# Three small edits in a two-layer recurrent and attention step: a weight remainder split one unit later, a norm's root by ScalarE, and three of four last scalings on VectorE

## The chip, the core and the metric

One core of a Trainium2 chip runs the whole program. Times are device microseconds of one execution. TensorE (PE) multiplies, VectorE (DVE), ScalarE (ACT) and GpSimd (POOL) do the elementwise work, each executing its own queue in order, and SyncE (SP) issues most DMAs. What counts is the median time of several executions of the program.

## What is computed

The reference is one step of a streaming encoder with two layers, in float32. Per layer:

```python
z = rms_norm(h, norm_w) @ w_in            # 8 parts of 1024 columns
o_r = rglru(xr, zr)                       # 8 independent blocks of 128 channels
o_a = diff_attention(q, k, v, za)         # 8 heads
h = h + (sigmoid(g_r) * (o_r @ w_proj_rnn) + sigmoid(g_a) * (o_a @ w_proj_att)) @ w_out
```

The recurrent branch (RG-LRU) of one block of 128 channels:

```python
xc = causal_conv(xr)                      # 4 taps
r = sigmoid(xc @ w_rg + b_rg); i = sigmoid(xc @ w_ig + b_ig)
a = exp(-8 * r * softplus(-lru_lambda))
h[t] = a[t] * h[t-1] + sqrt(1 - a[t]**2) * i[t] * xc[t]
```

At the end the rows of `h` go through a last `rms_norm` to `y_prompt` (512 tokens) and `y_sample` (64 tokens).

## The kernel before

Activations are kept transposed: 128 channels on the partitions, 592 tokens (64 sample, 16 meta, 512 prompt) along the row. Each float32 product is made of three matmuls on rounded parts: a weight `w` is split into `wh` (rounded copy, ACT, line 156) and `wl` (the rest, DVE or POOL, line 161), and data likewise.

`dense` (line 196) makes one block of 128 output channels. It works in two halves of 296 (or 288) tokens, and one such half, 24 matmuls, is called a unit here: about 3.3 us of PE. After a unit's matmuls the code hands its PSUM bank to an evacuation, then calls `step()`, then splits weights some pieces ahead. `step()` advances every generator in the list `active` to its next `yield`, the oldest generator first. The generators hold everything that runs beside the dense products, so each engine's queue is written out by hand: what stands earlier in a step stands earlier in the queue.

`rnn_steps` (line 762) is the generator of one RG-LRU block. Its stages, one for each unit, are called U0 to U13 here:

- U0: the gate weights `gw` are loaded by DMA; POOL makes the first tap of the convolution (`xc`, line 769) and two copies of three columns (lines 770 and 771).
- U1 to U3: DVE adds the other taps (line 774).
- U4: ACT rounds `xc` to `xh` (line 779) and `gw` to `gh` (line 780); POOL makes the rest `gl` (line 781).
- U5: DVE makes the rest `xl` (line 783).
- U6 and U7: PE makes the two gates, six matmuls each in the order `gh*xh`, `gh*xl`, `gl*xh` (line 790), and ACT takes their tanh (line 792).
- U8: ACT makes Exp, Tanh and Sqrt (lines 797 to 799), DVE a product (line 800).
- U9: DVE makes `a` (line 802), POOL finishes it (line 803).
- U10 and U11: DVE (lines 805 and 807).
- U12: DVE scans over time (lines 810 and 811), POOL copies two last states (lines 812 and 813).
- U13: DVE multiplies by the gate (line 817).

`chains()` (line 853) starts the next block four units or more after the last one, so U4 of a block falls into the step of U0 of the next, U5 into that of U9 of the block before and of U1 of the next, and U12 of a block into that of U4 of the second block after it. Blocks are numbered 0 to 7 in the first layer and 8 to 15 in the second. Before each block of `xr` POOL also fills the border columns of `xb` (lines 889 to 892).

The last stage of layer 1 multiplies by `w_out` in two parts, of 320 and of 256 tokens. Per block, DVE adds the residual (`hn`, line 1068) and scales it (`hx`, line 1069), ACT squares it (line 1074), POOL sums the squares (line 1076), and `to_tokens` (line 1027) transposes `hx` on PE and lets ACT copy the transposed block to `Y` (line 1034). After the second part `sums` (line 286) multiplies the two remaining sums, `acc` and the last `sq`, by ones on PE to get one sum of squares per token, all into one bank; `rstd` (line 281) makes the inverse root on DVE from a magic number and three Newton steps (lines 267 to 273); and `scale_out` (line 1042) scales `Y` and sends it out by DMA, in four pieces of 128 tokens x 512 columns: two on DVE with SP's queue, two on ACT with ACT's own queue.

Of the kernel before, what the change touches and what calls it, by code (L numbers as in the profile page):

```python
# [26 lines left out]
AF = mybir.ActivationFunctionType  # L27
OP = mybir.AluOpType
AX = mybir.AxisListType

D = 1024
# [6 lines left out]
EPS = 1e-6  # L38
# [8 lines left out]
def f32(ap):  # L47
    return ap.bitcast(FT)
# [39 lines left out]
def tile_kernel(ctx, tc, I, O):  # L88
    nc = tc.nc
    V, S, P, PE, SY = nc.vector, nc.scalar, nc.gpsimd, nc.tensor, nc.sync  # L90
# [19 lines left out]
    def ps_t():  # L110
        return ps.tile([128, 512], FT, name="pt")

    def ps_s():
        return ps.tile([128, 2, 512], FT, name="pss", bufs=2)
# [4 lines left out]
    def small(name, n, dt=FT, bufs=2):  # L119
        return sm.tile([128, n], dt, name=name, bufs=bufs)  # L120
# [110 lines left out]
    ones = cn.tile([128, 128], FT, name="ones")  # L231
# [49 lines left out]
    def rstd(ss, n=5, E=V):  # L281
        v = small("v5", 5)[:, :n]
        E.tensor_scalar(v, ss, 1.0 / D, EPS, op0=OP.mult, op1=OP.add)
        return rsqrt(v, n, E)

    def sums(xs, tiles, p=None, between=None):

        p = p or ps_t()
        for t, (c, n) in enumerate(tiles):
            for i, x in enumerate(xs):  # L290
                PE.matmul(p[:n, t:t + 1], x[:, c:c + n], ones[:, 0:1], start=(i == 0), stop=(i == len(xs) - 1))
        full = [t for t, (c, n) in enumerate(tiles) if n == 128]
        assert full == list(range(len(full)))
        if len(full) == len(tiles):
            return rstd(p[:, :len(tiles)], len(tiles))
        ss = small("ssl", 5)[:, :len(tiles)]
        V.memset(ss, 1.0)
        V.tensor_copy(ss[:, :len(full)], p[:, :len(full)])
        for t in range(len(full), len(tiles)):
            n = tiles[t][1]  # L300
            V.tensor_copy(ss[:n, t:t + 1], p[:n, t:t + 1])
        if between:
            between()
        return rstd(ss, len(tiles))
# [23 lines left out]
    def conv_w(l, k, j): return prm[:, 16 + 32 * l + 8 * k + j:16 + 32 * l + 8 * k + j + 1]  # L328
    def conv_b(l, j): return prm[:, 80 + 8 * l + j:80 + 8 * l + j + 1]
    def state_rnn(l, j): return prm[:, 144 + 8 * l + j:144 + 8 * l + j + 1]  # L330
    def state_conv(l, k, j): return prm[:, 160 + 24 * l + 8 * k + j:160 + 24 * l + 8 * k + j + 1]
    def half_brg(l, j): return hb[:, 8 * l + j:8 * l + j + 1]
    def half_big(l, j): return hb[:, 16 + 8 * l + j:16 + 8 * l + j + 1]
    def sp_m4(l, j): return spc[:, 0, 8 * l + j:8 * l + j + 1]
    def sp_p2(l, j): return spc[:, 1, 8 * l + j:8 * l + j + 1]
# [74 lines left out]
    for k in range(KT):  # L410
# [10 lines left out]
        for n in range(2):  # L421
            for i, (a, b) in enumerate(((0, hwh), (0, hwl), (1, hwh))):
                for hf, (c0, m) in enumerate(ALL):
                    PE.matmul(banks[n][hf][:, :m], wt[n][a][:, k], b[k][:, c0:c0 + m], start=(k == 0 and i == 0),  # L424
                              stop=(k == KT - 1 and i == 2))
# [336 lines left out]
    def rnn_steps(l, j, xb, zg, orr, NSt, rp):  # L762
        def rblk(name, dt=FT):
            return rp.tile([128, TW], dt, name=name, tag="r", bufs=9)

        gw = rp.tile([128, 2, 128], FT, name="gw", bufs=2)
        SY.dma_start(gw, I["gw"][l, j])
        xc = rblk("xc")
        P.tensor_scalar(xc, xb[:, 0:TW], conv_w(l, 0, j), conv_b(l, j), op0=OP.mult, op1=OP.add)
        P.tensor_copy(NSt[:, 0, j:24:8], xb[:, 528:531])  # L770
        P.tensor_copy(NSt[:, 1, j:24:8], xb[:, 595:598])
        for k in range(1, 4):
            yield
            V.scalar_tensor_tensor(xc, xb[:, k:k + TW], conv_w(l, k, j), xc, op0=OP.mult, op1=OP.add)
        yield
        gh = rp.tile([128, 2, 128], FR, name="gh", bufs=2)
        gl = rp.tile([128, 2, 128], FR, name="gl", bufs=2)
        xh, xl = rblk("xh", FR), rblk("xl", FR)
        S.activation(xh, xc, AF.Copy)
        S.activation(gh, gw, AF.Copy)  # L780
        P.tensor_tensor(gl, gw, f32(gh), op=OP.subtract)
        yield
        V.tensor_tensor(xl, xc, f32(xh), op=OP.subtract)
        yield
        tg = []
        for g, bias in ((0, half_brg(l, j)), (1, half_big(l, j))):
            p = ps_s()
            for i, (w, x) in enumerate(((gh, xh), (gh, xl), (gl, xh))):
                for hf in range(2):
                    PE.matmul(p[:, hf, :298], w[:, g], x[:, 298 * hf:298 * hf + 298], start=(i == 0), stop=(i == 2))  # L790
            t = rblk(f"tg{g}")
            S.activation(t.rearrange("p (a b) -> p a b", a=2), p[:, :, :298], AF.Tanh, bias=bias, scale=0.5)
            tg.append(t)
            yield
        v, u = tg
        e, q, a = rblk("e"), rblk("q"), v
        S.activation(e, v, AF.Exp, bias=sp_m4(l, j), scale=sp_m4(l, j))
        S.activation(v, v, AF.Tanh, bias=sp_p2(l, j), scale=sp_p2(l, j))
        S.activation(q, v, AF.Sqrt)
        V.scalar_tensor_tensor(u, u, 1.0, xc, op0=OP.add, op1=OP.mult)  # L800
        yield
        V.scalar_tensor_tensor(a, e, 1.0, v, op0=OP.add, op1=OP.mult)
        P.tensor_scalar(a, a, -1.0, 1.0, op0=OP.mult, op1=OP.add)
        yield
        V.scalar_tensor_tensor(e, e, 1.0, q, op0=OP.add, op1=OP.mult)
        yield
        V.scalar_tensor_tensor(u, e, 0.5, u, op0=OP.mult, op1=OP.mult)
        hs = e
        yield
        V.tensor_tensor_scan(hs[:, 0:528], a[:, 0:528], u[:, 0:528], 0.0, op0=OP.mult, op1=OP.add)  # L810
        V.tensor_tensor_scan(hs[:, 531:595], a[:, 531:595], u[:, 531:595], state_rnn(l, j), op0=OP.mult, op1=OP.add)
        P.tensor_copy(NSt[:, 0, 24 + j:25 + j], hs[:, 527:528])
        P.tensor_copy(NSt[:, 1, 24 + j:25 + j], hs[:, 594:595])
        yield
        o = orr[j] = rp.tile([128, T], FT, name="or", bufs=4) if j < 4 else blk("or")
        for c, n, t0 in (((0, 64, 531), (64, 528, 0)) if l == 0 else ((16, 64, 531), (80, 512, 16))):
            V.scalar_tensor_tensor(o[:, c:c + n], hs[:, t0:t0 + n], 0.5, zg[:, c:c + n], op0=OP.mult, op1=OP.mult)
# [11 lines left out]
    for l in range(DEPTH):  # L829
# [33 lines left out]
        for nm in order_rnn():  # L863
# [51 lines left out]
            if rp is None and not active:  # L915
# [5 lines left out]
                    lambda n, dt, i=i: rp.tile([128, T], dt, name=f"{n}{i}") for i in range(3)]))  # L921
# [96 lines left out]
        else:  # L1018
# [23 lines left out]
            def scale_out(t, y, i, E, q, c):  # L1042
                n = 64 if t == 4 else 128
                if E is S:
                    S.activation(Y[:n, t, c], Y[:n, t, c], AF.Copy, scale=y[:n, i:i + 1])
                else:
                    E.tensor_scalar(Y[:n, t, c], Y[:n, t, c], y[:n, i:i + 1], None, op0=OP.mult)
                dst = O["y_prompt"][0, 128 * t:128 * (t + 1), c] if t < 4 else O["y_sample"][0][:, c]
                q.dma_start(dst, Y[:n, t, c])

            def first_out(xs, tiles):
# [3 lines left out]
                for i, (t, c) in enumerate(tiles):  # L1055
                    scale_out(t, y, i, V, SY, slice(0, D))
                    yield

            for part, (c0, m, tiles) in enumerate(parts):
                acc = blk("acc")  # L1060
                xs = [acc]
                for j in range(KT):
                    load_h(part, j + 1)
                    hn, hx = blk("hn"), blk("hx")

                    def evac(hf, c0, m, p):
                        cs = slice(c0, c0 + m)
                        V.tensor_tensor(hn[:, cs], p[:, :m], hos[part, j][:, cs], op=OP.add)
                        V.tensor_scalar(hx[:, cs], hn[:, cs], fw[:, j:j + 1], None, op0=OP.mult)
                        if j == 0:  # L1070
                            S.activation(acc[:, cs], hn[:, cs], AF.Square)
                        else:
                            sq = blk("sq")
                            S.activation(sq[:, cs], hn[:, cs], AF.Square)
                            if j < KT - 1:
                                P.tensor_tensor(acc[:, cs], acc[:, cs], sq[:, cs], op=OP.add)
                            else:
                                xs.append(sq)

                    dense((l, f"out{'ab'[part]}{j}"), (mh, ml), evac, [(c0, m)])  # L1080
                    if part == 0 or j < KT - 1:
                        active.append(token_step(j, hx, tiles))
                if part == 0:
                    active.append(first_out(xs, tiles))
            y = sums(xs, [(c, 128) for t, c in tiles])
            to_tokens(KT - 1, hx, tiles)
            for g in range(2):
                c = slice(512 * g, 512 * g + 512)
                scale_out(2, y, 0, V, SY, c)
                scale_out(3, y, 1, S, S, c)  # L1090


_OUTS = [("y_prompt", (1, 512, 1024)), ("y_sample", (1, 64, 1024)), ("new_k", (DEPTH, NH, 128, T)),
# [76 lines left out]
```

## Time and profile before

| | |
|---|---|
| median of 3 runs | 1324.07 us (1323.75 to 1325.9) |
| the profiled execution | 1325.13 us |
| its span on the core | 1323.4 us |
| busy: PE, DVE, ACT, POOL | 1311.1, 969.1, 673.7, 375.7 us |
| matmuls | 9768 |

The span is what the profile of the core covers; the profiled execution takes 1.7 us more around it. Busy times are sums over all instructions of an engine; a matmul's end is modelled, so starts of successive matmuls say more of PE than its busy share.

### The profile page before, as it was taken

The page shows a single profiled execution, that of the slowest core. Times are in us where ns is not written, and L with a number is a line of the kernel's source. Part 1 is how long each engine was busy: PE and PEld are TensorE (multiplying, and loading weights), DVE is VectorE, ACT ScalarE, POOL GpSimd, SP SyncE. Part 2 cuts the span into 40 slices and gives each one's busy share as a digit, 9 for nine tenths or more (in the row PEclk, how much of TensorE's full clock was granted, in tenths as well). Part 3 has the DMA queues.
Part 4 walks back from the last instruction along what each step waited for, and adds up shares of the span by engine and source line. Part 5 has one row for each costly group of instructions (what it writes and reads, how often), then busy time and mean ns, then how long its engine had stood idle before and what let it go on. Part 6 is the DMA issues. An engine that isn't in the chain of part 4 may idle for free.

```text
span 1323.4 us, 26301 instructions
## 1 busy us (share of the span) xinstructions
PE 1311.1 (99%) x9768; PEld 1306.7 (99%) x9768; DVE 969.1 (73%) x2031; ACT 673.7 (51%) x1575; POOL 375.7 (28%) x736
## 2 busy tenths in 40 slices
PE   9999999999999999999999999999999999999997
PEld 9999999999999999999999999999999999999997
DVE  7998888874477886555568898998735789755576
ACT  5455555564336664423425555555632566553343
POOL 1224555442212331000212245445231143200011
PEclk9999999999999999999999999999999999999999
DMA  6557777776332221223443677777663222222254
GB/s 228 171 143 171 184 175 188 183 179 146 103 106 73 73 83 65 97 80 126 175 140 113 168 187 186 185 174 181 165 153 120 69 77 89 80 81 80 92 184 140
DMA packets 260575, 179.06 MB, mean 135 GB/s; under 512 B 177952, under 2 KB 222624, under 8 KB 260448
## 3 DMA queue, kind: packets, MB, share of 16 engines
q1 hardware_dynamic: 260016, 176.85, 47.5%
q8 instruction: 77, 1.26, 0.4%
q10 hardware_dynamic: 432, 0.53, 0.1%
q14 instruction: 50, 0.41, 0.1%
HBM read 132.37 MB, written 35.26 MB: 127 GB/s over the span
## 4 chain that ended last, share of the span: by engine, by line
PE 86%; issue 6%; DVE 3%; DMA 2%; POOL 1%; SPq 1%; ACT 0%; ACTq 0%; POOLq 0%; DVEq 0%
PE pd L208 72%; PE pss L478 2%; PE pss L481 2%; PE po L545 2%; PE pss L790 2%; PE pt L545 1%; DMA gw<-in_gw_dram 1%; PE pd L424 1%; DVE wl L161 1%; PE pt L543 1%; PE po L208 1%; PE pss L208 0%; PE pt L208 0%; PE pt L549 0%; PE pss L424 0%
## 5 line engine op out<-in xcount | busy, mean ns | idle before, releaser
L208 PE MATMUL pd<-hwh,wh 128*128 128x296 f32 (+1 forms) x1968 | 589.0, 299 | 1.4 <-DVE xs L664 1.3
L208 PE MATMUL pd<-hwh,wl 128*128 128x296 f32 (+1 forms) x1968 | 587.0, 298 | 0.7 <-DVE wl L161 0.7
L208 PE MATMUL pd<-hwl,wh 128*128 128x296 f32 (+1 forms) x1968 | 586.0, 298 | 0.0
L208 PEld LDWEIGHTS pd<-hwh,wh 128*128 128x128 f32 x1968 | 370.6, 188 | 2.0 <-DVE xs L664 1.1
L208 PEld LDWEIGHTS pd<-hwh,wl 128*128 128x128 f32 x1968 | 370.2, 188 | 1.2 <-DVE wl L161 1.2
L208 PEld LDWEIGHTS pd<-hwl,wh 128*128 128x128 f32 x1968 | 370.9, 188 | 0.0
L161 DVE TENSOR_TENSOR wl<-stg,wh 128x512 fp32r<-128x512 f32 x321 | 236.6, 741 | 0.3 <-ACT wh L156 0.2
L156 ACT ACTIVATE wh<-stg 128x512 fp32r<-128x512 f32 x364 | 221.7, 621 | 4.5 <-PE pss L208 1.6
L758 ACT ACTIVATE zg<-zt 128x296 f32<-128x296 f32 (+1 forms) x64 | 28.7, 449 | 157.6 <-DVE zt L757 151.2
L511 ACT ACTIVATE P<-pss,nm 128x400 f32<-128x400 f32 (+4 forms) x128 | 62.4, 492 | 81.8 <-DVE nm L508 78.0
L676 POOL TENSOR_TENSOR xc<-xc,xr 128x592 f32<-128x592 f32 x32 | 50.4, 1576 | 183.7 <-DMA xr<-xs 111.9
L161 POOL TENSOR_TENSOR wl<-stg,wh 128x512 fp32r<-128x512 f32 x43 | 59.6, 1386 | 112.1 <-ACT wh L156 100.7
L208 PE MATMUL pd<-oah,wl 128*128 128x296 f32 (+1 forms) x256 | 76.4, 298 | 0.8 <-DVE wl L161 0.8
L208 PE MATMUL pd<-mh,wh 128*128 128x296 f32 (+2 forms) x256 | 77.1, 301 | 0.0
L208 PE MATMUL pd<-oal,wh 128*128 128x296 f32 (+1 forms) x256 | 76.2, 298 | 0.0
L208 PE MATMUL pd<-mh,wl 128*128 128x296 f32 (+2 forms) x256 | 76.2, 298 | 0.0
L208 PE MATMUL pd<-orl,wh 128*128 128x296 f32 (+1 forms) x256 | 76.1, 297 | 0.0
L208 PE MATMUL pd<-oah,wh 128*128 128x296 f32 (+1 forms) x256 | 76.1, 297 | 0.0
L208 PE MATMUL pd<-orh,wl 128*128 128x296 f32 (+1 forms) x256 | 76.0, 297 | 0.0
L208 PE MATMUL pd<-orh,wh 128*128 128x296 f32 (+1 forms) x256 | 75.9, 296 | 0.0
L208 PE MATMUL pd<-ml,wh 128*128 128x296 f32 (+2 forms) x256 | 75.9, 296 | 0.0
L520 ACT ACTIVATE P<-pss,nm 128x528 f32<-128x528 f32 x32 | 22.5, 702 | 71.5 <-DVE nm L518 46.3
(262 smaller groups left out, 2545.7 us busy)
## 6 DMA issues: line engine op xcount, KB each, us to landing
stg<-in_w_dram SPq DMA_DIRECT2D x182, 512.0 KB, 3.7
pd<-AB SPq DMA_DIRECT2D x64, 160.0 KB, 3.7
PT<-pd SPq DMA_DIRECT2D x64, 160.0 KB, 3.7
xr<-xs SPq DMA_DIRECT2D x128, 74.0 KB, 4.3
od<-ob SPq DMA_DIRECT2D x64, 80.0 KB, 3.1
kv<-kv SPq DMA_DIRECT2D x64, 76.0 KB, 2.3
out_new_k_dram<-xc SPq DMA_DIRECT2D x16, 296.0 KB, 4.0
out_new_v_dram<-vT SPq DMA_DIRECT2D x16, 296.0 KB, 3.8
```

The costliest lines, as they stand in the source:

```text
L156: S.activation(hi, src, AF.Copy)
L161: E.tensor_tensor(lo, src, f32(hi), op=OP.subtract)
L208: PE.matmul(p[:, :m], a[:, k], b[k][:, c0:c0 + m], start=(i == 0), stop=(i == 23))
L424: PE.matmul(banks[n][hf][:, :m], wt[n][a][:, k], b[k][:, c0:c0 + m], start=(k == 0 and i == 0), stop=(k == KT - 1 and i == 2))
L478: PE.matmul(p[:nq, slot, :nn], qs[c][:, q0:q0 + nq], ks[c][:, k0:k0 + nn], start=True, stop=False)
L481: PE.matmul(p[:nq, slot, :nn], qlz[c][:, q0:q0 + nq], ks[c][:, k0:k0 + nn], start=False, stop=True)
L511: S.activation(pcs[i, cc][:nq, :n], p[:nq, cc, :n], AF.Exp, bias=nm[:nq, cc:cc + 1], accum_out=Z[:nq, cc, i:i + 1])
L520: S.activation(pcs[i, c][:, :528].rearrange("p (a b) -> p a b", a=2), p[:, :, :264], AF.Exp, bias=nm[:, :1], accum_out=Z[:, c, i:i + 1])
L545: PE.matmul(o, PT[0][:, j0 + j], vt[:, j], start=False, stop=(j == i))
L676: P.tensor_tensor(xc[x][:, :T], xc[x][:, :T], r[:, :T], op=OP.add)
L758: S.activation(zg[:, cs], zt[:, cs], AF.Tanh, scale=0.5)
L790: PE.matmul(p[:, hf, :298], w[:, g], x[:, 298 * hf:298 * hf + 298], start=(i == 0), stop=(i == 2))
```

## The change

`gl` is made by POOL in U5 instead of U4. In the last stage, a one-element Sqrt on ACT stands ahead of the two parts; the two last sums go to two banks of another PSUM tile, in the order acc, acc, sq, sq; the root of the last norm is ACT's Sqrt, DVE's reciprocal and one step of Newton; and three of the four last scalings are on DVE with SP's queue, one on ACT.

```diff
         S.activation(xh, xc, AF.Copy)
         S.activation(gh, gw, AF.Copy)
+        yield
         P.tensor_tensor(gl, gw, f32(gh), op=OP.subtract)
-        yield
         V.tensor_tensor(xl, xc, f32(xh), op=OP.subtract)
         yield
...
+            root = small("root", 1)
+            S.activation(root, ones[:, 0:1], AF.Sqrt)
             for part, (c0, m, tiles) in enumerate(parts):
...
-            y = sums(xs, [(c, 128) for t, c in tiles])
+            p = ps_s()
+            for i, x in enumerate(xs):
+                for t, (_, c) in enumerate(tiles):
+                    PE.matmul(p[:, t, 0:1], x[:, c:c + 128], ones[:, 0:1], start=(i == 0), stop=(i == 1))
             to_tokens(KT - 1, hx, tiles)
-            for g in range(2):
-                c = slice(512 * g, 512 * g + 512)
-                scale_out(2, y, 0, V, SY, c)
-                scale_out(3, y, 1, S, S, c)
+            v, y, a, b = [small(n, 2) for n in ("v5", "ny", "na", "nb")]
+            V.tensor_scalar(v, p[:, :, 0], 1.0 / D, EPS, op0=OP.mult, op1=OP.add)
+            S.activation(y, v, AF.Sqrt)
+            V.tensor_scalar(b, v, -0.5, None, op0=OP.mult)
+            V.reciprocal(y, y)
+            V.tensor_tensor(a, y, y, op=OP.mult)
+            V.tensor_tensor(a, a, b, op=OP.mult)
+            V.scalar_tensor_tensor(y, a, 1.5, y, op0=OP.add, op1=OP.mult)
+            for i, (g, E, q) in enumerate(((0, V, SY), (0, S, S), (1, V, SY), (1, V, SY))):
+                scale_out(2 + i % 2, y, i % 2, E, q, slice(512 * g, 512 * g + 512))
```

## Rows read from the trace of the kernel before

In rows of a timeline the columns are start (us), duration (us), engine, line, operation, output and inputs with their shapes, count, and in brackets the engine's idle time just before with what ended it.

**Rows 1.** The page: the span and its first part (busy us, share, instructions).

```profile
span 1323.4 us, 26301 instructions
PE 1311.1 (99%) x9768; PEld 1306.7 (99%) x9768; DVE 969.1 (73%) x2031; ACT 673.7 (51%) x1575; POOL 375.7 (28%) x736
```

**Rows 2.** The waits of PE over the whole span: who waited for whom, us in total, times, longest.

```profile
PE pd L208 <- DVE wl L161: 1.5, 4, 0.4
```

**Rows 3.** POOL's timeline around block 3 of the RG-LRU.

```profile
438.56 1.07 POOL L781 TENSOR_TENSOR gl<-gw,gh 128x256 fp32r<-128x256 f32 x1 [3.11 <-ACT gh L780]
439.61 0.84 POOL L769 TENSOR_SCALAR xc<-xb,prm 128x596 f32<-128x596 f32 x1
...
440.67 1.21 POOL L803 TENSOR_SCALAR tg<-tg 128x596 f32<-128x596 f32 x1
```

**Rows 4.** DVE's timeline at the same place, and one row from block 7's step.

```profile
437.55 0.78 DVE L802 SCALAR_TENSOR_TENSOR tg<-e,tg 128x596 f32<-128x596 f32 x1
...
440.48 0.85 DVE L774 SCALAR_TENSOR_TENSOR xc<-xb,prm,xc 128x596 f32<-128x596 f32 x1 [1.46 <-POOL xc L769]
441.26 1.16 DVE L161 TENSOR_TENSOR wl<-stg,wh 128x512 fp32r<-128x512 f32 x1
...
497.45 0.77 DVE L802 SCALAR_TENSOR_TENSOR tg<-e,tg 128x596 f32<-128x596 f32 x1
```

**Rows 5.** PE's timeline: the first matmuls with `gl` of blocks 2, 3 and 4, and PE's wait after block 3's gates.

```profile
425.00 0.44 PE L790 MATMUL pss<-xh,gl 128*128 128x298 f32 x2
...
439.76 0.46 PE L790 MATMUL pss<-xh,gl 128*128 128x298 f32 x2
...
441.83 0.30 PE L208 MATMUL pd<-hwl,wh 128*128 128x296 f32 x1
442.48 0.40 PE L208 MATMUL pd<-hwh,wl 128*128 128x296 f32 x1 [0.35 <-DVE wl L161]
442.71 0.30 PE L208 MATMUL pd<-hwh,wh 128*128 128x296 f32 x1
...
455.16 0.43 PE L790 MATMUL pss<-xh,gl 128*128 128x298 f32 x2
```

**Rows 6.** POOL's timeline around block 2 and around block 4; L812 and L813 copy states of an older block, L803 belongs to the block before.

```profile
420.03 0.66 POOL L813 COPY NSt<-e 128x1 f32<-128x1 f32 x1
...
421.93 2.01 POOL L769 TENSOR_SCALAR xc<-xb,prm 128x596 f32<-128x596 f32 x1
...
426.17 0.69 POOL L803 TENSOR_SCALAR tg<-tg 128x596 f32<-128x596 f32 x1
...
450.19 0.65 POOL L813 COPY NSt<-e 128x1 f32<-128x1 f32 x1
...
452.04 1.97 POOL L769 TENSOR_SCALAR xc<-xb,prm 128x596 f32<-128x596 f32 x1
...
455.39 1.14 POOL L803 TENSOR_SCALAR tg<-tg 128x596 f32<-128x596 f32 x1
```

**Rows 7.** POOL's timeline around blocks 6 and 7.

```profile
483.48 1.06 POOL L781 TENSOR_TENSOR gl<-gw,gh 128x256 fp32r<-128x256 f32 x1 [3.11 <-ACT gh L780]
484.51 1.13 POOL L803 TENSOR_SCALAR tg<-tg 128x596 f32<-128x596 f32 x1
...
498.31 1.82 POOL L803 TENSOR_SCALAR tg<-tg 128x596 f32<-128x596 f32 x1 [3.21 <-DVE tg L802]
500.16 1.19 POOL L781 TENSOR_TENSOR gl<-gw,gh 128x256 fp32r<-128x256 f32 x1
```

**Rows 8.** All instructions of the two lines on POOL: count, ns of the shortest, median and longest, start of the first and last.

```profile
L781 POOL TENSOR_TENSOR gl<-gw,gh x16: 735/904/1194, 390.5 to 1148.7; 128x256 fp32r<-128x256 f32 x16
L803 POOL TENSOR_SCALAR tg<-tg x16: 686/1134/1825, 410.5 to 1167.6; 128x596 f32<-128x596 f32 x16
```

**Rows 9.** One piece of the chain that ended last, near its end: start, us, what.

```profile
1314.74 0.84 PE pt L291 x6
```

**Rows 10.** The timeline of the last 9 us.

```profile
1315.60 0.16 DVE L283 TENSOR_SCALAR v<-pt 128x2 f32<-128x2 f32 x1 [0.98 <-PE pt L291]
...
1315.82 0.44 PE L1032 MATMUL pt<-ident,hx 128*128 128x128 f32 x2 [0.25 <-DVE v L283]
...
1316.29 0.38 ACT L1034 ACTIVATE Y<-pt 128x256 f32<-128x256 f32 x1 [1.34 <-PE pt L1032]
...
1317.57 0.16 DVE L273 SCALAR_TENSOR_TENSOR ny<-na,ny 128x2 f32<-128x2 f32 x1
1317.76 0.88 DVE L1047 TENSOR_SCALAR Y<-Y,ny 128x512 f32<-128x512 f32 x2
...
1319.71 0.34 ACTq L1049 DMA_DIRECT2D out_y_prompt_dram<-Y  x1
```

**Rows 11.** Two stretches at the end, in us from the span's start: their length, busy time of PE, PEld (weight loads), DVE, ACT and POOL with counts, granted clock, DMA share, GB/s.

```profile
1319.10:1321.90 2.80, 0.00 (x0) 0.00 (x0) 0.00 (x0) 0.58 (x1) 0.00 (x0) 0.50 0.99 372
1321.90:1323.40 1.50, 0.00 (x0) 0.00 (x0) 0.00 (x0) 0.00 (x0) 0.00 (x0) 0.50 0.02 5
```

**Rows 12.** Groups of ACT's instructions: busy us, mean ns; idle before.

```profile
L799 ACT ACT_TABLE_LOAD x16 | 20.5, 1283 | 0.4
...
L393 ACT ACTIVATE idle<-ones 128x1 f32<-128x1 f32 x1 | 0.2, 203 | 0.0
```

**Rows 13.** ACT's timeline at the start of the last stage.

```profile
1261.48 0.47 ACT L1071 ACTIVATE acc<-hn 128x320 f32<-128x320 f32 x1 [2.10 <-DVE hn L1068]
```

## Prediction

> **What bounds the kernel now.** I read the page first: PE is busy for 1311.1 of 1323.4 us [rows 1], so a microsecond that PE stands still is a microsecond of the result, and work on another engine costs only what PE waits for. Then PE's waits: in the whole span the largest entry is four waits for `wl` [rows 2]. I followed one of them back. At 442.48 PE starts a matmul 0.65 us after the one before it, where matmuls of a unit otherwise start 0.14 apart; the next starts 0.23 later [rows 5]. So this stall costs 0.51 + 0.09 = 0.60 us. Its `wl` is late because DVE stood still for 1.46 us before its convolution tap, waiting for POOL's first tap (line 769), and that tap stood in POOL's queue behind `gl`, which ran from 438.56 to 439.63 [rows 3, 4]. The other three follow the same order of instructions, one more in this layer and two in the next; I price the four at 2.5 us.
>
> Last I read the opposite side of the same queue: how early `gl` is. In block 3 it ends at 439.63 and PE uses it at 439.76 [rows 3, 5], without a wait: the margin is 0.13 us, while a unit is 3.3 us. There is hardly room to make it later.
>
> **Part 1: `gl` one unit later.** Removed is the tap's wait behind `gl`: POOL can make the tap up to several us earlier. The four stalls on `wl` go: **-2.5 us**.
>
> Added is what `gl` now stands behind. Its new step is U5, which is U9 of the block before it; the older generator comes first, so POOL's queue has `L803` of block j-1 and then `gl` of block j. `L803` waits for DVE's `L802`, which in block 3's step ends at 438.33 [rows 4]. PE wants `gl` at 439.76 [rows 5], 1.43 us after that, and in this time POOL must finish both instructions. PE's queue is in order: behind the waiting `gl` matmul stands the next whole unit, and every other engine's evacuations.
>
> *Blocks 1, 3, 6 and 9, 11, 14.* Here POOL is free when `L802` ends. Block 6 of the kernel before runs the same two instructions back to back in the other order, beside the same DVE work: 1.06 and 1.13 us [rows 7]. Swapped, with the start 0.09 us after `L802`'s end (498.22 to 498.31 in rows 4, 7) and 0.03 between them, `gl` ends 2.31 us after `L802`. PE resumes about 0.06 later (`wl` ended at 442.42, PE started at 442.48) and loses 0.09 on the next matmul. Stall: 2.31 + 0.06 + 0.09 - 1.43 = 1.03 us each, 6.2 for six.
>
> *Blocks 2, 4, 5 and 10, 12, 13.* Here POOL comes to `L803` late already, behind the tap and the copies. Without `gl` and the wait ahead of it, the tap of block 2's step starts at 420.69 instead of 421.93 [rows 6], so everything behind it moves 1.24 us forward: `L803` to 424.93, its end with 0.69 us to 425.62, `gl` with the shortest duration of 0.74 [rows 8] to 426.39. PE wants it at 425.00 [rows 5]: stall 1.39 + 0.15 = 1.54 us. In block 4, 455.39 - 1.20 = 454.19, plus 1.14, 0.03 and 0.74 is 456.10, against 455.16 [rows 5, 6]: 0.94 + 0.15 = 1.09. Block 5 has the durations of block 2. Mean 1.39, six of them 8.3 us.
>
> *Blocks 0, 7, 8 and 15* are not touched: block 0 and 8 have no older block ahead, and in block 7 `gl` stands behind `L803` already [rows 7].
>
> Such a stall should come back in every block: DVE waits for PE once or more between two blocks, so its lag behind PE begins anew each time, and a PE that was held up earlier does not start the next block with more room.
>
> Part 1 in sum: 6.2 + 8.3 - 2.5 = **+12.0 us**. Bounds. Shortest: both instructions at their shortest, 0.69 and 0.74 [rows 8], give `gl` 1.55 us after `L802`, a stall of 0.27 in the first kind and none in the second: +1.6 - 2.5 = -0.9 us. Longest: in block 7 the same pair took from 498.31 to 501.35 [rows 7], 3.13 us after `L802`: 1.85 us in the first kind, and with gl 0.45 and `L803` about 0.4 longer some 2.2 in the second, together 24.3 - 2.5 = +21.8 us. I stay with the swap: block 6 is the nearest row, the same neighbours on both engines.
>
> One rule makes the first kind worse. POOL and DVE hold each other up in the rows: `wl` takes 1.16 us beside `L803` [rows 3, 4] and `gl` 0.74 to 1.19 us [rows 8]. The Trainium skill ("SBUF — State Buffer", section "SBUF: two separate sides") says that the port pair which VectorE and GpSimd share is an exclusive lock, held for a whole instruction. The trace agrees with the direction: the two engines' instructions stretch each other. Taken strictly, it makes the rival "turns" below.
>
> **Part 2: the end.** The four remaining matmuls after the last `sq`, instead of six in 0.84 us [rows 9], bring `v` forward by 0.28 us, from 1315.60 to 1315.32, its end to 1315.48. The transposes no longer wait for `v` to free the bank [rows 10]: they start at about 1315.3 instead of 1315.82, and ACT's copy of `Y`, which stands ahead of the Sqrt in ACT's queue, at 1315.77 instead of 1316.29, until 1316.15. A small ACT instruction takes 0.20 us [rows 12]: Sqrt until 1316.35. Then four small DVE steps, each 0.195 us after the one before (nine of them and two others lie between 1315.60 and 1317.76): `y` is there at about 1317.15 instead of 1317.73. I take **-0.6 us**.
>
> The scalings: on ACT the last DMA was issued at 1319.71 [rows 10]; on DVE, 0.44 us for each piece, the last would be issued about 0.7 us earlier still. But from 1319.1 to 1321.9 the DMA engines were busy all the time, and after that hardly at all [rows 11]: the four pieces, 1.05 MB, moved at their full rate, and the first piece's start did not depend on the last issue. So the three on DVE bring nothing beyond the earlier `y`; if the last issue did bound, the end would gain 1.3 us in all, and if the Sqrt is costly it loses (below). `root` loads Sqrt's table, 1.28 + 0.2 us on ACT, at the start of the last stage, in a place where ACT is idle for 2.10 us [rows 12, 13]: nothing, and without that cover at most 1.5.
>
> **Sum.** +12.0 - 0.6 = +11.4 us. The profiled execution took 1325.13 us (span 1323.4 and 1.7 around it), so it becomes 1336.5; that execution is 1.06 above the median of 1324.07, so the median becomes **1335.5 us**, 0.9% slower. A measurement of this kernel tells about 0.2%, 2.65 us, from no change.
>
> **Rivals.**
> - *POOL is quick (other side).* If `L803` and `gl` together end within 1.4 us of `L802`'s end, PE does not wait, and the change brings -2.5 - 0.6 to -1.3: 1320.5 to 1321. For it: the shortest `L803` and `gl` sum to 1.43 us [rows 8]. Against it: these shortest times come when DVE is idle or reads PSUM, and behind `L802` DVE is busy; medians sum to 2.04. With the shortest everywhere it is 1324.07 - 0.9 - 0.6 = 1322.6. Chance 0.07.
> - *Half of it.* Stalls of 0.3 to 0.5 us in place of 1.0 to 1.5, when the tap and the copies on POOL, now earlier, fall into DVE's pauses: 1322 to 1326.7. Chance 0.15.
> - *Turns.* POOL and DVE take strict turns: `L803` waits until `xl` is done (0.7 after `L802`), DVE's tap waits for `L803` (0.69), `gl` waits for the tap (0.76) and takes 0.74: 2.9 us after `L802`, or the 3.13 of block 7 [rows 7]. Six stalls of 1.6 to 1.85 in the first kind, 9.6 to 11.1 instead of 6.2, and 2 us in the second: 1339 to 1345. Chance 0.12; its lower half is in the range.
> - *Sqrt's table is lost.* If ACT's squares in the last stage load another table, the last Sqrt waits for its own, 1.28 us [rows 12], on the path: the end is 0.7 slower instead of 0.6 faster, in all 1336.8. No row has a Square right after a Sqrt, so the trace can't exclude it. Chance 0.1, on top of the others. The Trainium skill ("ScalarE: Activation LUTs", section "Table sets: the hidden batching unit") lists relu, copy, identity and abs as present in every set and does not name Square there. It puts a switch at about 2.7 us with its drain; here the load row has 1.28 us.
>
> **How the numbers follow.** The forecast's own case (1327 to 1339) has 0.66. With 0.07 and 0.15 below and 0.12 above, a range from 1324.5 to 1341 leaves out about 0.2: the quick rival, half of the second, the upper half of "turns". Slower by over 0.2%: the forecast, "turns" and what is left above 1326.7, 0.78; within 0.2%: most of the half case and some of the quick one, 0.16; faster: 0.06.
>
> **What would show it.** Right: PE's waits list `gl` (L781) as the largest entry, about a dozen times of 1 us or more, in blocks 1 to 6 of each layer; `wl` has gone from them; `gl` follows `L803` in POOL's timeline; the tap is several us earlier; `y` about 0.6 us earlier relative to the last `sq`, one table load at `root` and none at the end; the DMAs of the end still full for 2.8 us. Wrong: `gl` ending before PE's `xl` matmuls, or stalls that do not recur in the second layer.

## Result and profile after

The changed kernel takes 1341.12 us (median; 1340.12 to 1342.86) against 1324.99 us of the kernel before on the same chip (1323.75 to 1326.94). The ratio is 1.0126, 95% interval 1.0113 to 1.0139: 16.1 us slower, where 11.4 were forecast. The profiled execution took 1342.86 us, the longest of the four.

The first part of the page of the changed kernel, against [rows 1]:

```profile
span 1341.1 us, 26284 instructions
PE 1315.0 (98%) x9768; PEld 1308.9 (98%) x9768; DVE 963.6 (72%) x2026; ACT 675.4 (50%) x1577; POOL 379.0 (28%) x736
```

The span grew by 17.7 us and PE's busy time by only 3.9. So most of the loss is PE standing still, and a few us are PE being busy for longer with the same 9768 matmuls; the second has a cause of its own, below.

PE's waits, largest entry (us in total, times, longest), against [rows 2]:

```profile
PE pss L790 <- POOL gl L782: 15.7, 12, 2.1
```

The four waits for `wl` are gone and twelve for `gl` are there, six in each layer. A wait costs PE a little more than its idle time. Counted as in the prediction (distance to the matmul before, less the usual 0.137 us, plus about 0.10 at the next), the twelve cost 18.9 us: 1.24 each in the mean of blocks 1, 3, 6, 9, 11, 14 (1.11 to 1.36); 1.02 in the mean of 4 and 12; 2.34 in 2, 5, 10, 13.

**The first kind.** POOL's, DVE's and PE's timelines of the changed kernel around block 3 (start us, us, engine, what), against [rows 3, 4, 5]:

```profile
440.06 1.59 POOL L769 TENSOR_SCALAR xc<-xb,prm 128x596 f32<-128x596 f32 x1
...
443.12 1.16 POOL L803 TENSOR_SCALAR tg<-tg 128x596 f32<-128x596 f32 x1 [0.73 <-DVE tg L802]
444.24 1.25 POOL L782 TENSOR_TENSOR gl<-gw,gh 128x256 fp32r<-128x256 f32 x1
```

```profile
442.26 0.77 DVE L802 SCALAR_TENSOR_TENSOR tg<-e,tg 128x596 f32<-128x596 f32 x1
442.95 0.77 DVE L783 TENSOR_TENSOR xl<-xc,xh 128x596 fp32r<-128x596 f32 x1
443.64 1.26 DVE L774 SCALAR_TENSOR_TENSOR xc<-xb,prm,xc 128x596 f32<-128x596 f32 x1
444.82 1.21 DVE L161 TENSOR_TENSOR wl<-stg,wh 128x512 fp32r<-128x512 f32 x1
```

```profile
445.54 0.55 PE L790 MATMUL pss<-xh,gl 128*128 128x298 f32 x2 [1.00 <-POOL gl L782]
```

`gl` follows `L803` and ends at 445.49, 2.46 us after `L802` (443.03); the forecast was 2.31. Read the ends of both engines in one list: `xl` 443.72, `L803` 444.28, tap 444.90, `gl` 445.49, `wl` 446.03. POOL and DVE take turns, each ending 0.54 to 0.62 us after the other. So the 1.25 us recorded for `gl` include its wait for its turn. The same 2.45 to 2.46 us lie between the ends of `L802` and `gl` in blocks 1, 9, 11, 4 and 12 too, and 2.36 in blocks 6 and 14; what differs more from block to block is when PE wants `gl`.

**The second kind.** The same around block 2, where the copies of three border columns (`L892`) stand ahead of `L803`, against [rows 6]:

```profile
423.52 0.68 POOL L892 COPY xb<-prm 128x1 f32<-128x1 f32 x1
424.13 0.75 POOL L892 COPY xb<-prm 128x1 f32<-128x1 f32 x1
424.82 0.81 POOL L892 COPY xb<-prm 128x1 f32<-128x1 f32 x1
425.60 1.14 POOL L803 TENSOR_SCALAR tg<-tg 128x596 f32<-128x596 f32 x1
426.71 1.24 POOL L782 TENSOR_TENSOR gl<-gw,gh 128x256 fp32r<-128x256 f32 x1
```

```profile
423.38 0.77 DVE L802 SCALAR_TENSOR_TENSOR tg<-e,tg 128x596 f32<-128x596 f32 x1
424.07 0.77 DVE L783 TENSOR_TENSOR xl<-xc,xh 128x596 fp32r<-128x596 f32 x1
424.75 0.83 DVE L774 SCALAR_TENSOR_TENSOR xc<-xb,prm,xc 128x596 f32<-128x596 f32 x1
425.50 0.69 DVE L161 TENSOR_TENSOR wl<-stg,wh 128x512 fp32r<-128x512 f32 x1
426.11 0.46 DVE L896 TENSOR_TENSOR xb<-pd,rb 128x296 f32<-128x296 f32 x1
426.48 0.88 DVE L805 SCALAR_TENSOR_TENSOR e<-e,q 128x596 f32<-128x596 f32 x1
```

A copy of one column ends at 424.20, 424.88 and 425.63, each time 0.04 to 0.05 us after a DVE instruction (424.15, 424.84, 425.58). Before each copy ends, DVE has had one whole instruction: 0.7 us for one column. Then `L803` ends 0.55 after `wl` and `gl` 0.59 after `L805`, 3.80 us after `L802`.

**The clock.** PE's timeline of the changed kernel after that wait, and three stretches there (length, busy us of PE, PEld, DVE, ACT, POOL with counts, granted clock, DMA share, GB/s):

```profile
428.00 0.55 PE L790 MATMUL pss<-xh,gl 128*128 128x298 f32 x2 [2.10 <-POOL gl L782]
...
428.87 0.45 PE L208 MATMUL pd<-hwh,wh 128*128 128x296 f32 x1
429.12 0.45 PE L208 MATMUL pd<-hwl,wh 128*128 128x296 f32 x1
```

```profile
425.50:428.00 2.50, 0.40 (x3) 0.15 (x3) 2.50 (x5) 0.00 (x0) 2.44 (x3) 1.00 0.00 0
428.70:432.10 3.40, 3.40 (x16) 3.40 (x16) 0.48 (x1) 2.48 (x3) 0.00 (x0) 0.50 0.59 193
432.10:435.50 3.40, 3.40 (x26) 3.40 (x26) 2.12 (x4) 1.62 (x3) 0.00 (x0) 1.00 0.01 5
```

PE was idle for 2.10 us and resumed at 428.00; from 428.7 to 432.1 the granted clock is 0.50, the level of 1.2 GHz, and matmuls start 0.247 us apart instead of 0.137. Some 14 matmuls lose 0.11 us each, about 1.5 us. The same comes after block 5 (by the starts of the slow matmuls, 480.18 to 483.35): 3.0 us in all, and the sum of the prediction has nothing for it.

**The end.** Timeline of the changed kernel from the last sums, its last stretches, and the group of the new table load, against [rows 9 to 13]:

```profile
1333.28 0.61 PE L1090 MATMUL pss<-ones,sq 128*128 128x1 f32 x4 [0.41 <-ACT sq L1076]
...
1333.92 0.16 DVE L1093 TENSOR_SCALAR v<-pss 128x2 f32<-128x2 f32 x1 [0.76 <-PE pss L1090]
...
1334.19 0.38 ACT L1034 ACTIVATE Y<-pt 128x256 f32<-128x256 f32 x1 [0.70 <-PE pt L1032]
1334.48 0.20 ACT L1094 ACTIVATE ny<-v 128x2 f32<-128x2 f32 x1
1334.70 0.17 DVE L1096 RECIPROCAL ny<-ny 128x2 f32<-128x2 f32 x1 [0.42 <-ACT ny L1094]
...
1335.49 1.28 DVE L1047 TENSOR_SCALAR Y<-Y,ny 128x512 f32<-128x512 f32 x3
```

```profile
1336.90:1339.70 2.80, 0.00 (x0) 0.00 (x0) 0.00 (x0) 0.00 (x0) 0.00 (x0) 0.50 0.99 370
1339.70:1341.10 1.40, 0.00 (x0) 0.00 (x0) 0.00 (x0) 0.00 (x0) 0.00 (x0) 0.50 0.00 0
```

```profile
L1060 ACT ACT_TABLE_LOAD x1 | 1.3, 1283 | 0.0
```

From the end of the last `sq` (1333.23) the span goes on for 7.87 us, before 8.71 (1314.69 to 1323.4; spans are printed to 0.1 us): about 0.8 saved, 0.6 forecast. The first scaling starts 2.26 us after that `sq`, before 3.07. The Sqrt at 1334.48 follows the copy with no table load.

### The profile page after: what moved, and what is told of

Read it like the earlier page. It is cut to its first block, busy times and chain, and to the rows that moved or that the text cites. A ratio compares the mean times of both kernels' runs of the same rounds, so it can differ in the third digit from the quotient of the medians.

```text
span 1341.1 us, 26284 instructions
## 1 busy us (share of the span) xinstructions
PE 1315.0 (98%) x9768; PEld 1308.9 (98%) x9768; DVE 963.6 (72%) x2026; ACT 675.4 (50%) x1577; POOL 379.0 (28%) x736
## 4 chain that ended last, share of the span: by engine, by line
PE 86%; POOL 5%; DVE 4%; issue 3%; DMA 1%; ACT 1%; SPq 0%; DVEq 0%; POOLq 0%; ACTq 0%
PE pd L208 73%; PE pss L481 2%; PE pss L478 2%; PE pss L790 2%; PE po L545 2%; POOL gl L782 1%; POOL xc L769 1%; PE pt L545 1%; POOL tg L803 1%; DVE e L810 1%; PE pt L543 1%; PE pt L549 1%; PE po L543 1%; PE pss L208 0%; PE pd L424 0%
## 5 line engine op out<-in xcount | busy, mean ns | idle before, releaser
L161 DVE TENSOR_TENSOR wl<-stg,wh 128x512 fp32r<-128x512 f32 x321 | 232.7, 728 | 0.3 <-ACT wh L156 0.2
L757 DVE TENSOR_TENSOR zt<-pd,rb 128x288 f32<-128x288 f32 (+1 forms) x62 | 28.5, 460 | 54.3 <-PE pd L208 54.0
```

The lines of the kernel that those rows point to most:

```text
L161: E.tensor_tensor(lo, src, f32(hi), op=OP.subtract)
L757: V.tensor_tensor(zt[:, cs], p[:, :m], rb[:, cs], op=OP.mult)
```

## Experiments

**Each part by itself.** The new end with `gl` in its old stage, and the old end with `gl` one unit later.

```diff
 (the changed kernel)
+        P.tensor_tensor(gl, gw, f32(gh), op=OP.subtract)
         yield
-        P.tensor_tensor(gl, gw, f32(gh), op=OP.subtract)
```

> The changed kernel with gl back in U4: only the new end. Theory (the slowdown is all in gl's place in POOL's queue): no wait of PE for gl, the four waits for wl are back, the last y about 0.8 us earlier after the last sq, the whole 0.8 us faster than before, which the timing can't tell from no change. Rival (the end costs too, by a table load or by three DMAs on one queue): no faster or up to 1.5 us slower.

```diff
 (the kernel before)
-        P.tensor_tensor(gl, gw, f32(gh), op=OP.subtract)
         yield
+        P.tensor_tensor(gl, gw, f32(gh), op=OP.subtract)
```

> The kernel before with gl moved to U5 and nothing else. Theory: 12 waits of PE for gl, about 15.7 us in all plus restarts, and about 17 us slower than before. Rival (the two parts act together): clearly less than 15 us.

PE's waits, the new end alone, then `gl` alone:

```profile
PE pd L208 <- DVE wl L161: 1.5, 4, 0.4
```

```profile
PE pss L790 <- POOL gl L782: 14.4, 12, 2.1
```

The end alone: 1323.31 us, ratio 0.9985 (0.9976 to 0.9993), 2.0 us (0.9 to 3.2) faster; its rows account for 0.8 of it. `gl` alone: 1340.09 us, ratio 1.0108 (1.0092 to 1.0125), 14.7 us slower by medians, where 17 were expected and clearly less than 15 was to be the rival's sign. The twelve waits come with `gl` alone and none of them with the end alone, so the loss belongs to `gl`. But the two parts add up to 12.6 us, and the changed kernel lost 16.1; with intervals of about 2 us on either side, whether the parts also act on each other is not settled. The rows show 1.3 us of the difference. With `gl` alone, blocks 2 and 5 wait as in the changed kernel and get the half clock again; in blocks 10 and 13 matmuls stand 1.76 and 1.75 us apart instead of 2.36, and the clock stays. There POOL's copy at L771 takes 0.19 us instead of 0.67, and `gl` ends 3.11 us after `L802` instead of 3.80: one turn less.

**`gl` later, but ahead of `L803`.** It is put off to the end of the same step, behind the new block's tap, copies and border columns.

```diff
 (the kernel before)
-        P.tensor_tensor(gl, gw, f32(gh), op=OP.subtract)
+        later(lambda: P.tensor_tensor(gl, gw, f32(gh), op=OP.subtract))
         yield
```

> The kernel before with gl issued between U4 and U5: in POOL's queue behind the next block's tap and copies and, in blocks 2, 5, 10 and 13, behind the border copies of xb, but ahead of L803. Theory (what makes gl late is what stands ahead of it, L803 above all): no waits in blocks 1, 3, 6, 9, 11, 14, where the tap runs before gh is there; at most 0.3 us in blocks 4 and 12; 0.5 to 2 us in blocks 2, 5, 10 and 13; the four waits for wl gone: 0 to 5 us slower than before. Rival (POOL is slowed by its neighbour DVE and gl is late wherever it stands in this step): waits of about 1 us in all twelve, 12 us or more slower.

PE's waits:

```profile
PE pss L790 <- POOL gl L781: 2.6, 4, 0.9
```

1325.46 us, ratio 1.0003 (0.9994 to 1.0012). The `wl` stalls go and four waits for `gl` come, in blocks 2, 5, 10, 13 alone. Being later than the tap costs `gl` next to nothing in the eight other blocks, so there it is `L803` ahead of it that costs. In these four, where copies and border columns stand ahead as well, 0.6 to 1.2 us of cost remain without `L803` ahead.

**The tap first.** With the new end, `gl` stays in U4, and the new block's U0 goes to the head of its step.

```diff
 (the changed kernel with gl back in U4)
-            done, since = 0, 99
-            while done < KT:
+            done, since, new = 0, 99, None
+            while done < KT or new:
                 since += 1
+                if new:
+                    next(new)
+                    active.append(new)
+                    new = None
                 if ready and since >= 4:
-                    active.append(rnn_steps(l, *ready.pop(0), orr, NSt, rp))
+                    new = rnn_steps(l, *ready.pop(0), orr, NSt, rp)
```

> The new end, gl back in U4, and U0 of a new block (its first tap, the two copies and the DMA of its gate weights) made at the head of the step instead of its end, so that POOL has the tap ahead of gl and nothing new ahead of L803. Theory: neither waits for gl nor the four for wl (2.5 us), the end 0.8 us shorter: 3.3 us faster than before, about 1321. Rival (the tap ahead of gl delays it as L803 did): waits for gl of 0.8 us or more in several blocks, 5 us or more slower.

1320.87 us, ratio 0.9969 (0.9957 to 0.9980): faster than both kernels, with no wait for `gl` or `wl` left. Against the end alone it is 2.4 us faster. In the trace of the end alone the four `wl` stalls, counted as in the prediction, cost 0.6 us each, so this is their price.

**The last scalings.** The new end alone, but two of the four on ACT.

```diff
-            for i, (g, E, q) in enumerate(((0, V, SY), (0, S, S), (1, V, SY), (1, V, SY))):
+            for i, (g, E, q) in enumerate(((0, V, SY), (0, S, S), (1, V, SY), (1, S, S))):
```

> The new end alone, but with two of the four last scalings on ACT with ACT's queue, as in the kernel before. Theory of the prediction: the DMA engines are full for 2.8 us at the end and the last issue does not bound, so from the start of the first scaling to the end of the span it is the same as with three on DVE (5.6 us, within 0.15). Rival: ACT's second scaling issues its DMA about 0.7 us later and the end is 0.4 to 0.7 us later.

From the first scaling to the end of the span, in one execution of each: 1316.77 to 1322.4, 5.63 us, and 1317.16 to 1322.7, 5.54 us with three on DVE; spans are printed to 0.1 us, so the two are the same. The last issue, though it comes later on ACT, is hidden by the DMA engines' 2.8 us.

**`L803` off POOL.**

```diff
 (the changed kernel)
-        P.tensor_scalar(a, a, -1.0, 1.0, op0=OP.mult, op1=OP.add)
+        S.activation(a, a, AF.Copy, bias=1.0, scale=-1.0)
```

> The changed kernel with L803 (a = 1 - a) on ACT instead of POOL, so that gl stands directly behind the border copies or an empty queue. Theory (gl is late by what stands ahead of it on POOL): in blocks 1, 3, 6, 9, 11, 14 PE does not wait for gl any more; in 2, 5, 10, 13 the border copies are still ahead and about 1 us of wait stays in each (2.2 in the changed kernel); block 4 and 12 at most 0.3. Waits for gl together about 4 us in place of 15.7; no drop of the clock behind them; time 1326 to 1330. Rival (gl itself is slow beside DVE wherever it stands, or ACT's evacuations become late by the extra instruction): waits of 0.5 us or more stay in the first kind, time 1333 or more.

PE's waits:

```profile
PE pss L790 <- POOL gl L782: 3.6, 4, 0.9
```

1325.76 us, just under what was expected; ratio to the kernel before 1.0008 (0.9999 to 1.0018). The eight other waits are gone, 1.15 to 1.19 us remain in blocks 2, 5, 10, 13, and no stretch of half clock follows them.

**The border copies off POOL.**

```diff
 (the changed kernel)
-                    P.tensor_copy(xb[:, 531 + k:532 + k], state_conv(l, k, j))
+                    S.activation(xb[:, 531 + k:532 + k], state_conv(l, k, j), AF.Copy)
```

> The changed kernel with the border copies of a block's state (L892, three columns) on ACT instead of POOL. Theory: the second kind of stall (blocks 2, 5, 10, 13) is long because these copies, 2.1 us beside DVE, stand ahead of L803 and gl: their waits fall from 2.2 us to 1.0 to 1.3, like those of the first kind, which do not change (1.0 to 1.2). Waits for gl 10 to 12 us in place of 15.7. If the length of the wait is what lowers the clock behind blocks 2 and 5 of the first layer, the clock stays at 1.00 there: 3 us more are saved; time 1333 to 1336. Rival: the second kind keeps 2 us (then it is L803 and gl themselves that are slow in that place) or the clock falls to 0.52 behind the shorter waits too.

The stretch behind block 2's wait, columns as above:

```profile
425.50:429.50 4.00, 4.00 (x29) 4.00 (x30) 3.06 (x6) 2.56 (x3) 0.00 (x0) 1.00 0.50 165
```

1333.52 us, ratio 1.0068 (1.0053 to 1.0083). In blocks 2, 5, 10, 13 the wait costs 0.96 to 1.02 us instead of 2.34, the others are unchanged, and the clock stays at 1.00. So the copies are what makes the second kind long, and without the long waits the half clock does not come. What stays open here is whether the copies are slow by POOL's own work on the columns or by the turns.

**The changed kernel again.**

> The changed kernel once more, unchanged, for a second profile. If the drop of the clock belongs to the place, blocks 2 and 5 of the first layer have it again (matmuls 247 ns apart for 3.2 us) and blocks 10 and 13 do not; if it depends on chance, other blocks have it or none. Waits for gl 15 to 16 us; time 1340 to 1342.5.

Two stretches of this execution, columns as above:

```profile
1081.60:1084.00 2.40, 0.43 (x4) 0.19 (x2) 2.40 (x5) 0.00 (x0) 2.40 (x3) 1.00 0.00 0
1084.30:1087.70 3.40, 3.40 (x16) 3.40 (x16) 0.98 (x2) 2.56 (x3) 0.00 (x0) 0.50 0.55 193
```

1342.29 us, the same twelve waits, but the half clock now follows blocks 10 and 13 of the second layer and not 2 and 5 of the first. It belongs to the long wait and not to a place, but not every long wait has it. What picks two of the four stays open.

**One copy of three columns.** Still on POOL, the same columns in one instruction; then also with `L803` on ACT, as above.

```diff
 (the changed kernel)
-                for k in range(3):
-                    P.tensor_copy(xb[:, 531 + k:532 + k], state_conv(l, k, j))
+                P.tensor_copy(xb[:, 531:534], prm[:, 160 + 24 * l + j:177 + 24 * l + j:8])
```

> The changed kernel with the three one-column border copies (L892) made as one copy of three columns, still on POOL. Theory (turns: beside DVE instructions with two inputs in SBUF each POOL instruction ends right behind one whole DVE instruction, however small it is): one copy costs one turn of 0.7 us instead of three (2.1 us), POOL reaches L803 1.4 us earlier in blocks 2, 5, 10, 13 and gl ends 2.4 to 2.5 us after L802 there as in the first kind. Waits of the second kind 1.0 to 1.25 us in place of 2.35, all others unchanged, the clock stays at 1.00; waits for gl 10 to 12 us in all; time 1333 to 1335. Rival (what is slow is POOL's reading of these columns, in proportion to their number): the one copy takes about 2 us and nothing changes, 1340 to 1342.

> The last one and L803 on ACT as well. Theory of turns: after the one copy ends, at about the end of L802, gl needs one turn more, behind xl: it ends 1.25 to 1.35 us after L802, 0.1 us ahead of PE's need at 1.42. No waits for gl in any block, none for wl, no drop of the clock: 1320.5 to 1322, the new end and the four wl stalls saved. Rival (gl late by other work in U5 too): waits of 0.3 us or more stay in blocks 2, 5, 10, 13: 1323 or more.

POOL's timeline around block 2 with the one copy:

```profile
423.87 0.67 POOL L891 COPY xb<-prm 128x3 f32<-128x3 f32 x1
424.59 1.15 POOL L803 TENSOR_SCALAR tg<-tg 128x596 f32<-128x596 f32 x1
425.70 1.24 POOL L782 TENSOR_TENSOR gl<-gw,gh 128x256 fp32r<-128x256 f32 x1
```

and POOL's and DVE's with `L803` on ACT too, where `L802` ends at 421.63:

```profile
421.00 0.68 POOL L891 COPY xb<-prm 128x3 f32<-128x3 f32 x1
421.64 1.28 POOL L782 TENSOR_TENSOR gl<-gw,gh 128x256 fp32r<-128x256 f32 x1
```

```profile
420.85 0.78 DVE L802 SCALAR_TENSOR_TENSOR tg<-e,tg 128x596 f32<-128x596 f32 x1
```

One copy of three columns takes 0.67 us, as long as one of one column beside DVE: here 0.7 us is the price of an instruction, not of its columns. The first kernel takes 1333.75 us, ratio 1.0072 (1.0057 to 1.0087); `gl` ends 2.45 us after `L802` in block 2, as in the first kind, the wait of the second kind costs 0.97 to 1.02 us, and the clock stays. In the second, `gl` ends 1.29 us after `L802`, one turn instead of two, PE waits neither for `gl` nor for `wl`, and the time is 1321.01 us, ratio 0.9973 (0.9963 to 0.9983). That is 3.6 us faster than the kernel before; the two gains by their rows, 2.5 and 0.8, add up to 3.3. With no work left behind which `gl` would wait, the changed place does no harm.

## Why the prediction was right or wrong

- **Direction and mechanism: right.** `gl` behind `L803` is late in the twelve blocks named, in both layers, and not in 0, 7, 8, 15; `wl` has gone from PE's waits; the tap starts 2.20 us before `L802` in block 3's step and not 2.06 after it. "Quick", "half of it" and "Sqrt's table" fell: no wait costs under 0.9 us, and one table load stands at `root`, none at the end.
- **First kind: a little small.** 1.24 us for 1.03, 1.3 us over six. "The same neighbours" was true of blocks 6 and 14 alone: there `wl` follows `xl` on DVE, `gl` ends 2.36 us after `L802` for the 2.31 forecast, and block 6's wait costs 1.11. In the other four the tap stands between `xl` and `wl`, and it is 2.45. The swap kept 1.06 us for `gl` from block 6, where it went first; behind `L803` it takes 1.25 in block 3. Block 4 and 12: 1.02 for 1.09.
- **Second kind: the step that failed.** 1.54 us was forecast for blocks 2, 5, 10, 13, and it is 2.34: 3.2 us over four. `L803`'s start came out right, 5.07 us after `L812`'s for the forecast 5.14 (424.93 less 419.79), but by luck: the shorter tap (1.29 us for 2.01) and copy at L770 (0.24 for 0.73) made up for the three border copies (2.11 us for 0.82). Then I gave `L803` and `gl` their shortest durations, 0.69 and 0.74, and they took 1.14 and 1.24, 0.95 more. The rows of block 2 before with these durations [rows 6, 8] come from moments in which DVE worked on L896, which reads PSUM, while they ran or when they began; moved 1.24 us forward, the two stand beside `wl` and L805. Durations of POOL had to be taken for the new neighbours, as I did, nearly, for the first kind.
- **The clock: left out, the other step that failed.** 3.0 us in the profiled execution, in none of the terms. I had priced what PE waits and not what it is granted afterwards.
- **"Turns" was right in kind and too dear.** Strict turns were a rival with 2.9 us from `L802` to `gl`'s end. The order of the ends is strictly that, and the two kernels with one copy came out by it. But a turn adds 0.54 to 0.62 us and not the 0.69 to 0.76 that I took from durations, so it is 2.45. The swap's 2.31 came from rows in which the turns already were: the rival and the swap were one mechanism, priced from two places. The Trainium skill ("SBUF — State Buffer", section "SBUF: two separate sides") has it as a lock held for the whole instruction, against DVE instructions with two inputs in SBUF. The trace agrees: the one DVE instruction in the list around block 2 that reads PSUM, L896, ended at 426.57 without ending a turn of POOL's.
- **`wl`, 2.5 us: right** (2.4 between the end alone and the tap first).
- **The end: -0.8 for -0.6.** The sums brought `v` forward nearly as forecast: it starts 0.69 us after `sq`, before 0.91. ACT's copy of `Y` started 0.27 us after `v` (0.45 forecast) and let the Sqrt follow 0.29 after its own start (0.38 forecast). Three scalings on DVE bring nothing, as forecast. By medians the end alone is worth 2.0 us, with 0.9 as the near end of the interval; what lies between, no row shows.

With the measured terms the sum is 18.9 + 3.0 - 2.5 - 0.8 = 18.6 us, against 17.7 in the span of the same execution and 16.1 between medians. The two kernels without long waits, the border copies off POOL and the one copy, tell what the clock is worth between medians. They lose 8.9 and 9.1 us, 7.0 to 7.2 less than the changed kernel, and their waits cost 5.4 less; the rest, 1.6 to 1.8 us, is an estimate for the clock, with intervals of about 2 us on each time. Their rows too come out higher than the whole, 10.2 us for 8.9 and 9.1, so that part of the difference is not the clock's; it stays open.

## What to carry to other kernels

Price a moved POOL instruction by what DVE does at the new place: where DVE has work with two SBUF inputs, each POOL instruction waited here for one DVE instruction, so merge small copies or give them to ACT. Before an operation is made later, read how early it is (here 0.13 us) and what stands ahead of it in the queue of its new step; moving the tap ahead instead saved the same `wl` stalls at no price. And a stall of TensorE may cost more than its length, as behind the four waits of 2.1 us here: look at the granted clock behind it.

## What the runs showed of the hardware that was not expected

- A POOL copy of one column, 128x1, took 0.68 to 0.81 us beside DVE, and one of three columns 0.67. The same three copies took 0.82 us in block 3's step of the changed kernel, where DVE's L883, which reads PSUM, ran beside two of them, and 2.11 in block 2's.
- Behind waits of 2.1 us the granted clock fell to 0.50 for 3.4 us, and matmuls stood 0.240 to 0.247 us apart: in two of four such places in both profiles of the changed kernel, and in both such places with `gl` alone. Behind the waits of up to 1.5 us for `gl` it stayed at 1.00 in all profiles here.
- A Sqrt after Squares and copies on ACT needed no table load: one load of 1.28 us at `root` held to the end of the kernel. The Trainium skill ("ScalarE: Activation LUTs", section "Table sets: the hidden batching unit") does not name Square among those present in every set; here Square did not take Sqrt's table away.
